# Four-tile dot products, a per-tile gather allowance and a rearranged end in a hard-max attention kernel

## Chip, cores, metric

One core of one Trainium2 chip. The metric is the device time of one execution in microseconds; medians are quoted. A ratio is the mean time of one kernel's fast runs over that of the other's fast runs of the same rounds, so it is not quite the ratio of the medians quoted beside it.

"Session" here means one set of runs made one after the other on one chip, with runs of the kernel before among them. Chips differed from session to session. A session in which the kernel before takes about 467 us is called **quick**, and one in which it takes over 500 us **late**. A run's label "fast" or "slow" is given against runs of the same kernel in the same session. All ratios below are taken within a session; where single figures of two sessions stand side by side, the runs are named.

## The reference

```python
# q, k, v: 4 x 4096 x 128, fp32
logits = np.matmul(q, k.transpose(0, 2, 1))
best = np.argmax(logits, axis=-1)
return v[b_idx, best, :]
```

For every query, find the key with the largest dot product and return that key's row of v.

## The kernel before

A tile is 128 queries; there are T = 128 tiles. For each tile, TensorE computes screening scores of groups of four keys (pd, psn), ScalarE turns them into A and E, VectorE folds them into W and takes the eight best (TOP). That gives one candidate group per query. GpSimd then gathers the group's three key differences (kg, 128 rows of 768 bytes), VectorE computes three dot products per query (prod, p1, p2, D), picks the best of the four keys (pick), and GpSimd gathers the row of v (vr), which is stored. Queries too close to call are flagged and recomputed exactly, once for tiles 0 to 63 within the loop and once for 64 to 127 at the end.

Each engine gets its own list of operations. The Python generators below only decide the order of these lists: a group's dots are placed into VectorE's list some tiles after its gathers went into GpSimd's list.

```python
# ... cut ...
def gather(c, t0, n):                     # n = 2 tiles
    # ... cut: cand_t[c] is allocated at a chunk's first tile
    x = cand_t[c][:, t0 - c0:t0 - c0 + n]
    nc.vector.tensor_scalar(out=x, in0=TOP.bitcast(U32)[:, t0:t0 + n, 0], ...)   # cand
    kg = rp.tile([P, n, 3, P], FP16, tag=f"kg{n}", name=f"kg_{t0}", bufs=8)
    for j in range(n):
        near_q.append(lambda j=j: nc.gpsimd.indirect_dma_start(out=kg[:, j]..., in_offset=IOA(ap=x[:, j:j + 1], axis=0)))
    near_q.append(mark)                   # mark: done.add(("kg", t0))
    start(dots(c, t0, n), "dots", c)

def dots(c, x, m):
    yield "until", lambda: ("kg", x) in done, 1 if x >= TAIL else 2     # tiles to wait after the mark
    nc.vector.tensor_tensor(out=prod, in0=kg, in1=natq[...], op=OP.mult)
    yield "dve",
    nc.vector.tensor_tensor(out=p1, in0=prod[:, :, :, 0:64], in1=prod[:, :, :, 64:128], op=OP.add)
    # ... cut: p2 alike, then D by tensor_reduce

def issue(it):                            # what GpSimd gets in tile it
    while near_q and (n < 1 + (it >= T - 28 and len(near_q) > 2) or near_q[0] in marks):
        ...                               # one kg gather (two near the end)
    # ... cut
    take_late(2 if n == 0 and len(late_q) > 4 or it >= T - 24 and it % 2 == 0 else 1)   # one vr gather

# ... cut: in tile it: screen, fold, step (one operation of each live generator), top, gathers(it - 3), step, issue
TAIL = T - 24
```

GpSimd's list is therefore kg, vr, kg, vr.

Of the kernel before, what the change touches and what calls it, by code (L numbers as in the profile page):

```python
# [20 lines left out]
QSCALE = 128.0  # L21
TAU = 8.0
NEAR = 0.5
LATE = 8


@with_exitstack
def kernel(ctx, tc, q, k, v, out):
# [202 lines left out]
    def top(t):  # L231
        nc.vector.max(out=TOP[:, t, :], in_=W_t[t % NW].bitcast(FP32))  # L232
# [6 lines left out]
    def gather(c, t0, n):  # L239
        c0, c1 = chunks[c]  # L240
        if t0 == c0:
            cand_t[c] = sp.tile([P, c1 - c0], U32, tag=f"cand{c1 - c0}", name=f"cand_{c}", bufs=6)
        x = cand_t[c][:, t0 - c0:t0 - c0 + n]
        nc.vector.tensor_scalar(out=x, in0=TOP.bitcast(U32)[:, t0:t0 + n, 0], scalar1=IDX, scalar2=IDX,
                                op0=OP.bitwise_and, op1=OP.bitwise_xor)
        kg = rp.tile([P, n, 3, P], FP16, tag=f"kg{n}", name=f"kg_{t0}", bufs=8)
        assert len(kg_t) < 8
        kg_t[t0] = kg
        for j in range(n):
            near_q.append(lambda j=j: nc.gpsimd.indirect_dma_start(  # L250
                out=kg[:, j].rearrange("p f d -> p (f d)"), out_offset=None, in_=k16[t0 // NQT],
                in_offset=IOA(ap=x[:, j:j + 1], axis=0)))
        mark = lambda: done.add(("kg", t0))
        marks.add(mark)
        near_q.append(mark)
        start(dots(c, t0, n), "dots", c)

    def dots(c, x, m):
        c0 = chunks[c][0]
        d = D_t[c % 4]  # L260
        b = x // NQT
        yield "until", lambda: ("kg", x) in done, 1 if x >= TAIL else 2
        kg = kg_t.pop(x)
        prod = rp.tile([P, m, 3, P], FP16, tag=f"prod{m}", name=f"prod_{x}")
        nc.vector.tensor_tensor(out=prod, in0=kg, in1=natq[b % 2][:, x - b * NQT:x - b * NQT + m, :].unsqueeze(2).to_broadcast([P, m, 3, P]),  # L265
                                op=OP.mult)
        yield "dve",
        p1 = rp.tile([P, m, 3, 64], FP16, tag=f"p1{m}", name=f"p1_{x}")
        nc.vector.tensor_tensor(out=p1, in0=prod[:, :, :, 0:64], in1=prod[:, :, :, 64:128], op=OP.add)  # L269
        yield "dve",  # L270
        p2 = rp.tile([P, m, 3, 32], FP16, tag=f"p2{m}", name=f"p2_{x}")
        nc.vector.tensor_tensor(out=p2, in0=p1[:, :, :, 0:32], in1=p1[:, :, :, 32:64], op=OP.add)  # L272
        yield "dve",
        nc.vector.tensor_reduce(out=d[:, x - c0:x - c0 + m, 1:4], in_=p2, axis=AX_X, op=OP.add)  # L274
        done.add(("dot", x))

    def pick(c, t0, t1):
        n = t1 - t0
        b, qt = t0 // NQT, t0 % NQT
        d = D_t[c % 4][:, 0:n, :]  # L280
        yield "until", lambda: all(("dot", x) in done for x in range(t0, t1, 2)), 0
        cand = cand_t.pop(c)
        mx = sp.tile([P, n, 1], FP32, tag=f"mx{n}", name=f"mx_{c}")
        nc.vector.tensor_reduce(out=mx[:, :, 0], in_=d, axis=AX_X, op=OP.max)
        yield "dve",
        near = sp.tile([P, n, 4], FP32, tag=f"near{n}", name=f"near_{c}")
        nc.vector.scalar_tensor_tensor(out=near, in0=d, scalar=NEAR, in1=mx.to_broadcast([P, n, 4]),
                                       op0=OP.add, op1=OP.is_ge)
        yield "dve",
        sel = sp.tile([P, n, 4], FP32, tag=f"sel{n}", name=f"sel_{c}")  # L290
        nc.vector.tensor_tensor(out=sel, in0=near, in1=iota8.unsqueeze(1).to_broadcast([P, n, 4]), op=OP.mult)
        yield "dve",
        nc.vector.tensor_reduce(out=CNT[:, t0:t1], in_=sel, axis=AX_X, op=OP.add)
        done.add(("cnt", c))
        yield "cnt",
        win = sp.tile([P, n], U32, tag=f"win{n}", name=f"win_{c}")
        nc.vector.scalar_tensor_tensor(out=win, in0=CNT[:, t0:t1], scalar=float(b * Sk - 8), in1=cand, op0=OP.add, op1=OP.add)
        for i in range(0, n, 4):
            put_values(c, i, n, win, out[b].rearrange("(p t) d -> p t d", p=P)[:, qt + i:qt + i + 4])
# [21 lines left out]
    def flag_segment(t0, t1, ready, stored):  # L321
# [41 lines left out]
        nc.vector.scalar_tensor_tensor(out=posn, in0=iota_r[:, 0:8], scalar=bs, in1=val, op0=OP.add, op1=OP.mult)  # L363
        yield "dve", 0.17
        OH = fp.tile([P, 8, P], BF16, tag="OH", name=f"OH_{t0}")
        nc.vector.tensor_tensor(out=OH, in0=iota_h.unsqueeze(1).to_broadcast([P, 8, P]),
                                in1=posn.unsqueeze(2).to_broadcast([P, 8, P]), op=OP.is_equal)
        yield "dve", 0.17
        rec2 = fp.tile([P, 8, 2], BF16, tag="rec2", name=f"rec2_{t0}")
        nc.vector.tensor_copy(out=rec2[:, :, 0], in_=e8)  # L370
        yield "dve", 0.17
# [269 lines left out]
    def step(it):  # L641
        quick = it >= TAIL
        waiting = [s for s in live if s["kind"] == "dots" and ready(s, it)]
        quota = 2 if len(waiting) > 1 else 1
        for s in list(live):
            if s["kind"] == "dots":
                if quota and advance(s, it, False):
                    quota -= 1
            else:
                if advance(s, it, False) and quick and s["kind"] == "pick" and s in live:  # L650
                    advance(s, it, False)

    rest = [0]
# [1 line left out]
    def take_late(n):  # L655
        while n > 0 and late_q:
            g = late_q.pop(0)
            n -= g not in stores
            g()
        while late_q and late_q[0] in stores:  # L660
            wait_q.append((clock[0] + 2, late_q.pop(0)))
# [7 lines left out]
    def issue(it):  # L669
        n = 0  # L670
        clock[0] = it
        put_out(it)
        while near_q and (n < 1 + (it >= T - 28 and len(near_q) > 2) or near_q[0] in marks):
            g = near_q.pop(0)
            n += g not in marks
            g()
        if fast and it >= rest[0]:
            fast.pop(0)()
            rest[0] = it + 3
        take_late(2 if n == 0 and len(late_q) > 4 or it >= T - 24 and it % 2 == 0 else 1)  # L680

    def gathers(t):
        for c, (t0, t1) in enumerate(chunks):
            if t0 <= t < t1 and ((t - t0) % 2 or t == t1 - 1):
                x = t0 + (t - t0) // 2 * 2
                gather(c, x, t - x + 1)
            if t == t0:
                start(pick(c, t0, t1), "pick", c)
        if t % 8 == 7:
            put_rec(t - 7, t + 1)  # L690
        if t == SEGS[1] - 1:
            last = [c for c, x in enumerate(chunks) if x[1] == t + 1][0]
            start(flag_segment(0, t + 1, lambda: ("cnt", last) in done, lambda: ("out", last) in done), "flags")

    TAIL = T - 24
    units = []
    for b in range(1, B):
        x = b * NQT
# [1 line left out]
    for it in range(T):  # L700
        b, qt = it // NQT, it % NQT
        if it < 8:
            load_part(1, it)
        elif 10 <= qt < 18:
            load_part(b + 1, qt - 2)
        elif 18 <= qt < 26:
            load_part(b + 2, qt - 18)
        open_units = [u for u in units if u[1] <= it]
        if open_units:
            u = min(open_units)  # L710
            units.remove(u)
            assert it <= u[0]
            u[2](*u[3:])
        if it == 1:
            turn_q(0, 4, 8)
        if it in (1, 2, 3):
            turn_q(0, it * 8, it * 8 + 8)
        elif qt >= 16 and qt % 2 == 0 and b + 1 < B:
            turn_q(b + 1, (qt - 16) * 2, (qt - 14) * 2)
        if it > 0:  # L720
            screen(it)
        if it >= 1:
            fold(it - 1)
        if it == 1:
            put_k(0, 1)
        if it % NQT in (9, 13):
            put_k(it // NQT + 1, it % NQT // 13)
        step(it)
        if it >= 2:
            top(it - 2)  # L730
        if 3 <= it <= TAIL:
            gathers(it - 3)
        if it >= TAIL:
            gathers(it - 2)
        step(it)
        issue(it)

    def flush():
        while near_q:
            near_q.pop(0)()  # L740
# [4 lines left out]

    screen(T)
    top(T - 2)
    fold(T - 1)
    top(T - 1)
    gathers(T - 2)  # L750
    gathers(T - 1)
    flush()
    assert not [s for s in live if s["kind"] == "flags"] and not fast
# [15 lines left out]
    for p in [s for s in live if s["kind"] == "pick"]:  # L769
        c = p["c"]  # L770
        dot = [s for s in live if s["kind"] == "dots" and s["c"] == c]
        while dot:
            two, dot = dot[:2], dot[2:]
            drain(two)
        last = c == len(chunks) - 1
        if last:
            flags_first(T // 2, T)
        drain([p], "cnt" if last else None)
    flags_last(T // 2, T, lambda: drain([p]), late_now)
    man.__exit__(None, None, None)  # L780
# [30 lines left out]
```

## Time and profile before

| | us |
|---|---|
| three timed runs | 506.16, 503.34, 513.95 |
| the profiled execution | 467.3 (span 465.5) |

These two rows do not fit together: the profile shows an execution 36 to 47 us faster than the timed runs.

From the page of before: the busy line, and the busy tenths of VectorE and the granted TensorE clock in 40 slices of the span.

```profile
PE 380.2 (82%) x1834; PEld 168.3 (36%) x1834; DVE 417.8 (90%) x825; ACT 376.8 (81%) x437; POOL 318.1 (68%) x345
...
DVE  2689999999999999999999999999998999998330
...
PEclk9999999999999999999999999999999999995555
```

VectorE is full from the fourth slice almost to the end, and the granted clock is full until the screening is done (1.00 to 418.3 us, 0.5 after that). The table of windows of before says the same by stage (columns: stretch and its length, busy us and instructions of PE, PEld, DVE, ACT and POOL, granted clock, DMA share, GB/s; PE is TensorE, DVE VectorE, ACT ScalarE, POOL GpSimd):

```profile
40.00:120.00 80.00, 76.63 (x378) 34.39 (x377) 80.00 (x135) 78.18 (x96) 53.52 (x59) 1.00 0.58 107
120.00:240.00 120.00, 112.72 (x550) 50.41 (x549) 118.23 (x202) 114.75 (x138) 89.96 (x95) 1.00 0.54 112
240.00:360.00 120.00, 107.05 (x500) 46.48 (x499) 117.72 (x236) 108.95 (x123) 89.91 (x90) 1.00 0.43 104
```

VectorE is busy 80.0 of 80 us, then 118.2 and 117.7 of 120; ScalarE and TensorE follow. The groups of instructions of before that matter (busy us, mean ns, then idle time of the engine just before them and what ended it):

```profile
L228 DVE SCALAR_TENSOR_TENSOR W<-psn,E 128x1024 int16<-128x1024 f32 x128 | 166.0, 1297 | 7.0 <-ACT E L215 5.5 <-PE psn L212 1.5
...
L250 POOL DMA_INDIRECT kg<-k,cand x128 | 127.4, 995 | 85.1 <-issue 26.6 <-DVE p L269 23.5 <-DVE cand L244 17.9
...
L265 DVE TENSOR_TENSOR prod<-kg,natq 128x768 f16<-128x768 f16 x64 | 34.9, 546 | 3.9 <-DMA kg<-k,cand 3.9
```

Keep two of these numbers in mind: W waits 7.0 us in all, and prod waits 3.9 us for the kg transfer. VectorE's timeline of before, late in the loop (start us, duration us, engine, line, operation), shows how its operations follow each other:

```profile
404.61 0.17 DVE L244 TENSOR_SCALAR cand<-TOP 128x2 uint32<-128x2 uint32 x1
404.68 0.34 DVE L274 TENSOR_REDUCE D<-p 128x6 f32<-128x192 f16 x1
404.95 1.30 DVE L228 SCALAR_TENSOR_TENSOR W<-psn,E 128x1024 int16<-128x1024 f32 x1
406.13 0.54 DVE L265 TENSOR_TENSOR prod<-kg,natq 128x768 f16<-128x768 f16 x1
406.60 1.22 DVE L232 MAX8 TOP<-W 128x8 f32<-128x1024 f32 x1
```

Start to start, W costs 1.18 us and prod 0.47. A fixed part of about 0.06 us per operation can be read from cand, which does next to nothing (404.61 to 404.68 here; start to start, 0.058 us is the most frequent value in this trace). That this is a fixed part is my estimate; the trace of after agrees with it: there p1 takes 0.265 us from start to start over two tiles and 0.464 over four (medians), 0.07 less than twice.

### The profile page before, as it was taken

Reading aid. Unit: us, or ns where it says so; the run is one execution under the profiler, and the core shown is the slowest. Engines: PE = TensorE matmul, PEld = TensorE weight load, DVE = VectorE, ACT = ScalarE, POOL = GpSimd, SP = SyncE. Lnnn points to the kernel's source line nnn. Section 1 sums busy time; section 2 is a strip of 40 time slices with the busy share of each in tenths; the row PEclk is TensorE's granted clock in tenths of the full one; section 3 lists DMA queues with packets and bytes.
Section 4 is the critical chain, followed back from the end, with each engine's and each line's share of the span. In section 5 each row is a group of like instructions: output and inputs, shape, how many; then the busy total and the mean of one; then the engine's idle time right before and its main releaser. Section 6 shows DMA issues by size and latency. Waiting matters only on the chain.

```text
span 465.5 us, 6396 instructions
## 1 busy us (share of the span) xinstructions
PE 380.2 (82%) x1834; PEld 168.3 (36%) x1834; DVE 417.8 (90%) x825; ACT 376.8 (81%) x437; POOL 318.1 (68%) x345
## 2 busy tenths in 40 slices
PE   8999999998999889999998889998998888850100
PEld 4444444443444344444443334443333333320000
DVE  2689999999999999999999999999998999998330
ACT  2999999999999989999997889999998888840000
POOL 8233557877677888776678876677777777767730
PEclk9999999999999999999999999999999999995555
DMA  7934576853325877943235653423432333322320
GB/s 130 227 66 96 107 103 97 139 120 85 80 76 135 148 140 128 121 126 81 79 98 137 129 116 94 100 80 87 110 101 79 86 86 99 87 71 68 94 74 4
DMA packets 43624, 47.54 MB, mean 102 GB/s; under 512 B 25000, under 2 KB 33451, under 8 KB 43584
## 3 DMA queue, kind: packets, MB, share of 16 engines
q0 software_dynamic: 18752, 30.97, 33.7%
q1 hardware_dynamic: 24832, 16.13, 13.1%
q8 instruction: 14, 0.23, 0.2%
q14 instruction: 26, 0.21, 0.2%
HBM read 39.59 MB, written 12.19 MB: 111 GB/s over the span
## 4 chain that ended last, share of the span: by engine, by line
DVE 31%; issue 23%; ACT 13%; PE 13%; DMA 9%; POOL 7%; POOLq 0%; DVEq 0%; ACTq 0%
DVE W L228 14%; ACT A L202 10%; PE psn L193 5%; DVE TOP L232 5%; PE psn L212 4%; DMA kg<-k,cand 4%; ACT E L215 4%; DMA vr<-in_v_dram,win 3%; DVE prod L265 3%; PE pd L193 3%; POOL kg L250 3%; POOL vr L304 2%; DVE D L274 2%; DVE p L269 2%; DMA natk<-in_k_dram 2%
## 5 line engine op out<-in xcount | busy, mean ns | idle before, releaser
L202 ACT ACTIVATE A<-pd 128x1024 f16<-128x1024 f32 x256 | 258.6, 1041 | 23.0 <-PE pd L193 22.7
L250 POOL DMA_INDIRECT kg<-k,cand x128 | 127.4, 995 | 85.1 <-issue 26.6
L228 DVE SCALAR_TENSOR_TENSOR W<-psn,E 128x1024 int16<-128x1024 f32 x128 | 166.0, 1297 | 7.0 <-ACT E L215 5.5
L193 PE MATMUL pd<-kT,qT 128*128 128x512 f16 x512 | 151.8, 378 | 15.7 <-ACT A L202 14.8
L193 PE MATMUL psn<-kT,qT 128*128 128x512 f16 x512 | 151.8, 378 | 15.3 <-ACT A L202 7.9
L304 POOL DMA_INDIRECT vr<-in_v_dram,win x128 | 136.6, 1067 | 39.0 <-issue 37.5
L193 PEld LDWEIGHTS <-qT 128*128 128x128 f16 x1024 | 98.4, 97 | 163.9 <-issue 76.0
L232 DVE MAX8 TOP<-W 128x8 f32<-128x1024 f32 x128 | 155.8, 1217 | 0.0
L212 PE MATMUL psn<-A,identh 128*128 128x512 f16 x512 | 152.1, 378 | 0.0
L215 ACT ACTIVATE E<-psn 128x1024 int16<-128x1024 f32 x128 | 132.2, 1033 | 5.0 <-PE psn L212 5.0
L212 PEld LDWEIGHTS <-identh 128*128 128x128 f16 x512 | 49.6, 97 | 60.8
L265 DVE TENSOR_TENSOR prod<-kg,natq 128x768 f16<-128x768 f16 x64 | 34.9, 546 | 3.9 <-DMA kg<-k,cand 3.9
L269 DVE TENSOR_TENSOR p<-prod 128x384 f16<-128x384 f16 x64 | 22.3, 349 | 0.1
L274 DVE TENSOR_REDUCE D<-p 128x6 f32<-128x192 f16 x64 | 21.5, 336 | 0.1
L173 ACT ACTIVATE kT<-uk 128x256 f16<-128x256 f32 x48 | 20.1, 419 | 0.9 <-PE uk L170 0.9
L64 POOL DMA_DIRECT2D natk<-in_k_dram x27 | 16.1, 599 | 0.9 <-POOLq L795 0.8
L67 POOL DMA_DIRECT2D natq<-in_q_dram x27 | 16.3, 605 | 0.2
L169 PE MATMUL uk<-identh,natk 128*128 128x128 f16 x96 | 15.8, 218 | 0.6 <-ACT A L202 0.6
L272 DVE TENSOR_TENSOR p<-p 128x192 f16<-128x192 f16 x64 | 15.7, 245 | 0.0
L464 PE MATMUL fp_e<-n_e,tri 128*128 128x1 f32 x2 | 0.6, 361 | 16.7 <-DVE n_e L462 16.7
L170 PEld LDWEIGHTS <-natk 128*128 128x128 f16 x96 | 9.3, 97 | 7.7 <-issue 5.3
L169 PEld LDWEIGHTS <-natk 128*128 128x128 f16 x96 | 9.3, 97 | 5.6
(147 smaller groups left out, 133.5 us busy)
## 6 DMA issues: line engine op xcount, KB each, us to landing
out_dram<-vr SPq DMA_DIRECT2D x32, 256.0 KB, 2.2
natq<-in_q_dram POOLq DMA_DIRECT2D x26, 128.0 KB, 3.2
k<-kd SPq DMA_DIRECT2D x8, 384.0 KB, 4.2
natk<-in_k_dram POOLq DMA_DIRECT2D x24, 128.0 KB, 3.9
kg<-k,cand POOLq DMA_INDIRECT x128, 2.8
vr<-in_v_dram,win POOLq DMA_INDIRECT x128, 2.8
natq<-in_q_dram POOLq DMA_DIRECT2D x1, 768.0 KB
natk<-in_k_dram POOLq DMA_DIRECT2D x1, 512.0 KB, 5.2
```

Source lines behind the costliest of these rows:

```text
L169: nc.tensor.matmul(out=o, lhsT=natk[b % 2][:, h, 4 * m + x, :], rhs=identh, start=True, stop=False)
L193: nc.tensor.matmul(out=ps[:, n * 512:(n + 1) * 512], lhsT=qT[b % 2][:, qt * P:(qt + 1) * P], rhs=kT[b % 2][:, u * 1024 + n * 512:u * 1024 ...
L202: nc.scalar.activation(out=A, in_=ps, func=AF.Abs)
L212: nc.tensor.matmul(out=ps[:, n * 512:(n + 1) * 512], lhsT=identh, rhs=A[:, n * 512:(n + 1) * 512], start=False, stop=True)
L215: nc.scalar.activation(out=E, in_=ps, func=AF.Relu, scale=QSCALE)
L228: nc.vector.scalar_tensor_tensor(out=W_t[t % NW].bitcast(I16)[:, 1::2], in0=ps, scalar=QSCALE, in1=E, op0=OP.mult, op1=OP.max)
L232: nc.vector.max(out=TOP[:, t, :], in_=W_t[t % NW].bitcast(FP32))
L250: near_q.append(lambda j=j: nc.gpsimd.indirect_dma_start(out=kg[:, j].rearrange("p f d -> p (f d)"), out_offset=None, in_=k16[t0 // NQT], ...
L265: nc.vector.tensor_tensor(out=prod, in0=kg, in1=natq[b % 2][:, x - b * NQT:x - b * NQT + m, :].unsqueeze(2).to_broadcast([P, m, 3, P]), op ...
L269: nc.vector.tensor_tensor(out=p1, in0=prod[:, :, :, 0:64], in1=prod[:, :, :, 64:128], op=OP.add)
L274: nc.vector.tensor_reduce(out=d[:, x - c0:x - c0 + m, 1:4], in_=p2, axis=AX_X, op=OP.add)
L304: late_q.append(lambda j=j: nc.gpsimd.indirect_dma_start(out=vr[:, j, :], out_offset=None, in_=v_flat, in_offset=IOA(ap=win[:, i + j:i + j ...
```

## The change

The intent: fewer fixed costs on the full engine, VectorE, by doing the dots of four tiles in one operation up to tile 72 (products still over two); with one dot operation of such a group per tile; an allowance per tile that lets GpSimd issue two kg gathers and as many vr gathers as fit; and a shorter end. The core of the diff:

```diff
-LATE = 8
+LATE = 7
+NKG = 6
@@ gather
-        kg = rp.tile([P, n, 3, P], FP16, tag=f"kg{n}", name=f"kg_{t0}", bufs=8)
+        kg = rp.tile([P, 4, 3, P], FP16, tag="kg", name=f"kg_{t0}", bufs=NKG)[:, 0:n]
@@ dots
-        yield "until", lambda: ("kg", x) in done, 1 if x >= TAIL else 2
+        gap = ("wait", 1) if m == 4 else ("dve",)
+        yield "until", lambda: ("kg", x) in done, 2 if m < 4 and x < TAIL else 1
-        nc.vector.tensor_tensor(out=prod, in0=kg, in1=natq[...], op=OP.mult)
-        yield "dve",
+        h = min(m, 2)
+        for i in range(0, m, h):
+            nc.vector.tensor_tensor(out=prod[:, i:i + h], in0=kg[:, i:i + h], in1=natq[...], op=OP.mult)
+            yield gap
@@ issue
-        while near_q and (n < 1 + (it >= T - 28 and len(near_q) > 2) or near_q[0] in marks):
+        while near_q and (n < 1 or near_q[0] in marks or it >= 16 and n < 2):
...
-        take_late(2 if n == 0 and len(late_q) > 4 or it >= T - 24 and it % 2 == 0 else 1)
+        if it < 16: ...
+        busy = 0.45 if 10 <= qt < 18 and b + 1 < B or 18 <= qt < 26 and b + 2 < B else 0.0
+        room[0] = min(room[0] + 2.35 - busy, 3.0) - n
+        while room[0] >= 1 and late_q:
+            take_late(1)
+            room[0] -= 1
@@ gathers
-            if t0 <= t < t1 and ((t - t0) % 2 or t == t1 - 1): ...
+            m = 4 if t1 <= T - 56 else 2 if t < T - 2 else 1
+            if t0 <= t < t1 and (t - t0) % m == m - 1:
+                gather(c, t - m + 1, m)
@@
-    TAIL = T - 24
+    TAIL = T - 38
@@ main loop: gathers now after the second step, always for tile it - 2
@@ cut: flag segment advanced twice per step, its OH in four pieces; the last chunk drained
@@      one group at a time, with the first flag operations moved ahead of its last two groups
```

More of the change, by code (lines that the diff above doesn't have):

```diff
@@ L245, in gather @@
                                 op0=OP.bitwise_and, op1=OP.bitwise_xor)
-        kg = rp.tile([P, n, 3, P], FP16, tag=f"kg{n}", name=f"kg_{t0}", bufs=8)
-        assert len(kg_t) < 8
+        kg = rp.tile([P, 4, 3, P], FP16, tag="kg", name=f"kg_{t0}", bufs=NKG)[:, 0:n]
+        assert len(kg_t) < NKG
         kg_t[t0] = kg
@@ L261, in dots @@
         b = x // NQT
-        yield "until", lambda: ("kg", x) in done, 1 if x >= TAIL else 2
+        gap = ("wait", 1) if m == 4 else ("dve",)
+        yield "until", lambda: ("kg", x) in done, 2 if m < 4 and x < TAIL else 1
         kg = kg_t.pop(x)
-        prod = rp.tile([P, m, 3, P], FP16, tag=f"prod{m}", name=f"prod_{x}")
-        nc.vector.tensor_tensor(out=prod, in0=kg, in1=natq[b % 2][:, x - b * NQT:x - b * NQT + m, :].unsqueeze(2).to_broadcast([P, m, 3, P]),
-                                op=OP.mult)
-        yield "dve",
-        p1 = rp.tile([P, m, 3, 64], FP16, tag=f"p1{m}", name=f"p1_{x}")
+        prod = rp.tile([P, 4, 3, P], FP16, tag="prod", name=f"prod_{x}")[:, 0:m]
+        h = min(m, 2)
+        for i in range(0, m, h):
+            nc.vector.tensor_tensor(out=prod[:, i:i + h], in0=kg[:, i:i + h],
+                                    in1=natq[b % 2][:, x + i - b * NQT:x + i + h - b * NQT, :].unsqueeze(2).to_broadcast([P, h, 3, P]),
+                                    op=OP.mult)
+            yield gap
+        p1 = rp.tile([P, 4, 3, 64], FP16, tag="p1", name=f"p1_{x}")[:, 0:m]
         nc.vector.tensor_tensor(out=p1, in0=prod[:, :, :, 0:64], in1=prod[:, :, :, 64:128], op=OP.add)
-        yield "dve",
-        p2 = rp.tile([P, m, 3, 32], FP16, tag=f"p2{m}", name=f"p2_{x}")
+        yield gap
+        p2 = rp.tile([P, 4, 3, 32], FP16, tag="p2", name=f"p2_{x}")[:, 0:m]
         nc.vector.tensor_tensor(out=p2, in0=p1[:, :, :, 0:32], in1=p1[:, :, :, 32:64], op=OP.add)
@@ L274, in dots @@
         nc.vector.tensor_reduce(out=d[:, x - c0:x - c0 + m, 1:4], in_=p2, axis=AX_X, op=OP.add)
-        done.add(("dot", x))
+        done.update(("dot", i) for i in range(x, x + m))
     def pick(c, t0, t1):
@@ L280, in pick @@
         d = D_t[c % 4][:, 0:n, :]
-        yield "until", lambda: all(("dot", x) in done for x in range(t0, t1, 2)), 0
+        yield "until", lambda: all(("dot", x) in done for x in range(t0, t1)), 0
         cand = cand_t.pop(c)
@@ L365, in flag_segment @@
         OH = fp.tile([P, 8, P], BF16, tag="OH", name=f"OH_{t0}")
-        nc.vector.tensor_tensor(out=OH, in0=iota_h.unsqueeze(1).to_broadcast([P, 8, P]),
-                                in1=posn.unsqueeze(2).to_broadcast([P, 8, P]), op=OP.is_equal)
-        yield "dve", 0.17
+        for z in range(4):
+            nc.vector.tensor_tensor(out=OH[:, 2 * z:2 * z + 2], in0=iota_h.unsqueeze(1).to_broadcast([P, 2, P]),
+                                    in1=posn[:, 2 * z:2 * z + 2].unsqueeze(2).to_broadcast([P, 2, P]), op=OP.is_equal)
+            yield "wait", 1
         rec2 = fp.tile([P, 8, 2], BF16, tag="rec2", name=f"rec2_{t0}")
@@ L649, in step @@
             else:
-                if advance(s, it, False) and quick and s["kind"] == "pick" and s in live:
+                if advance(s, it, False) and (quick or s["kind"] == "flags") and s in live:
                     advance(s, it, False)
@@ L678, in issue @@
             fast.pop(0)()
-            rest[0] = it + 3
-        take_late(2 if n == 0 and len(late_q) > 4 or it >= T - 24 and it % 2 == 0 else 1)
+            rest[0] = it + 2
+            n += 1
+        if it < 16:
+            take_late(2 if n == 0 and len(late_q) > 4 else 1)
+            return
+        b, qt = it // NQT, it % NQT
+        busy = 0.45 if 10 <= qt < 18 and b + 1 < B or 18 <= qt < 26 and b + 2 < B else 0.0
[3 more added lines that the diff above has]
+            room[0] -= 1
+    room = [0.0]
     def gathers(t):
         for c, (t0, t1) in enumerate(chunks):
-            if t0 <= t < t1 and ((t - t0) % 2 or t == t1 - 1):
-                x = t0 + (t - t0) // 2 * 2
-                gather(c, x, t - x + 1)
+            m = 4 if t1 <= T - 56 else 2 if t < T - 2 else 1
+            if t0 <= t < t1 and (t - t0) % m == m - 1:
+                gather(c, t - m + 1, m)
             if t == t0:
@@ L730 @@
             top(it - 2)
-        if 3 <= it <= TAIL:
-            gathers(it - 3)
-        if it >= TAIL:
+        step(it)
+        if it >= 2:
             gathers(it - 2)
-        step(it)
         issue(it)
@@ L747 @@
     top(T - 2)
+    gathers(T - 2)
+    flush()
     fold(T - 1)
     top(T - 1)
-    gathers(T - 2)
     gathers(T - 1)
@@ L771 @@
         dot = [s for s in live if s["kind"] == "dots" and s["c"] == c]
+        last = c == len(chunks) - 1
         while dot:
-            two, dot = dot[:2], dot[2:]
+            if last and len(dot) == 2:
+                flags_first(T // 2, T)
+            two, dot = (dot[:1], dot[1:]) if last else (dot[:2], dot[2:])
             drain(two)
-        last = c == len(chunks) - 1
-        if last:
-            flags_first(T // 2, T)
         drain([p], "cnt" if last else None)
```

## The prediction

> **What bounds it now.** In the table of windows (profile of before, 465.5 us) VectorE is busy 100% of 40 to 160 us and about 98% of 160 to 400; ScalarE is next (94 to 99% to 240 us), TensorE third at granted clock 1.00. In the timeline, W operations follow each other every 2.74 and 3.11 us in turn; eight tiles with their pick take 23.9 us, 2.99 per tile. That is VectorE's own work, start to start: W 1.19, TOP 1.14, and per pair of tiles prod 0.46, p1 0.26, p2 0.16, D 0.25, cand 0.06. ScalarE needs about 3 x 0.91 plus a key unit of about 0.3 every second tile, 2.9: little room beneath. The tail, last W at 418.8 to the end, is a serial chain: last gathers, dots, pick, flags, eight value gathers, FR, FK, FV, branch, store.
>
> The timed runs (503 to 514) are about 40 us slower than the profiled one (467.3). [...]
>
> **What changes.**
> 1. Tiles 0 to 71: four tiles cost 2 prod + one p1, p2, D, cand (0.92 + 0.46 + 0.26 + 0.45 + 0.06 = 2.15 us) instead of 2.38. Only four fixed costs of about 0.06 us go. Over 18 groups: -4 us of VectorE, on the path at full clock, nearly none if TensorE bounds.
> 2. GpSimd issues the same 256 gathers, in bursts, 1.31 us each: no gain in itself.
> 3. Tiles 90 to 125: dots follow their gather after two tiles instead of (mostly) three. From cand's start to the second gather's landing: 0.43 + 1.31 + 2.83 = 4.6 us (tail of the timeline). VectorE's work from cand to prod there: 4.0 us, 4.3 with a pick. So 0.3 to 0.6 us stall per pair, 18 pairs: +5 to +8 us at full clock; hidden if tiles take 3.3 us or more. Before's 2 to 3 us of kg stalls inside the loop should go.
> 4. End: tile 127 gathers alone, 126 earlier (-1.3), dots over one tile (-0.7), two flag operations before the wait (-0.7); seven instead of eight value gathers between last kg and FR. FR comes about 3 us earlier after the last W; one value gather now sits behind FV and gives 1.3 back: -1.5 to -3.
> 5. Flag segment twice as fast through the loop, its OH in four pieces: +0.2.
>
> Sum at full clock: -4 - 2.5 - 2 + 6.5 = about -2; with TensorE the bound: -2 to -5 (end, smoother VectorE).
>
> **Predicted: 502 us, range 493 to 511; faster by over 2% 0.14, within 2% 0.80, slower 0.06.**
>
> **Right or wrong in the profile.** W to W over tiles 20 to 70 falls from 2.99 to about 2.93; VectorE instructions fall by about 60; prod waits on the kg transfer in the last 40 tiles (several us, 3.9 before); last W to FR issue 13 to 14 us instead of 16.5; last W to end 44 to 45.
>
> **What would make it wrong.** Something else slowing the timed runs: if GpSimd or gather latency, bursts and the shorter distance cost much more; if small VectorE bursts stall TensorE there, the smoother order gains over 2%. Kg landing faster than 2.8 us would remove step 3's loss: 1.5% in the profile.

-4 (step 1), -2.5 (the kg stalls of before in the loop, step 3), -2 (the end, step 4) and +6.5 (step 3) make -2; the +0.2 of step 5 is not in it. The predicted 502 lies 4 us under 506, the median of the three timed runs.

## The result, and the profile after

| | before | after |
|---|---|---|
| median us, first session | 506.56 (4 runs) | 530.94 (4 runs, 528.53 to 534.28) |
| ratio | | 1.051, 95% interval 1.042 to 1.060 |
| profiled | 467.3 | 534.3 |

The change made the kernel 5% slower; 531 lies outside the predicted range, and the forecast was "within 2%". The profile after is of one of the timed runs, so it is of the late kind and must not be held against the quick profile of before without care. From the page of after, the lines that answer to those shown:

```profile
PE 398.8 (75%) x1834; PEld 171.1 (32%) x1834; DVE 419.3 (79%) x761; ACT 380.8 (72%) x437; POOL 311.8 (59%) x345
...
DVE  3679999747789989839799989684998598899420
...
PEclk9999999968999999969998999996999799996555
```

The same windows of after:

```profile
40.00:120.00 80.00, 69.19 (x323) 30.12 (x322) 69.71 (x94) 67.41 (x83) 50.76 (x56) 0.92 0.56 104
120.00:240.00 120.00, 100.16 (x462) 43.38 (x461) 98.69 (x137) 97.34 (x115) 74.18 (x80) 0.94 0.45 96
240.00:360.00 120.00, 98.59 (x465) 42.55 (x464) 106.51 (x201) 97.74 (x114) 71.70 (x75) 0.99 0.39 89
```

And the same groups of after:

```profile
L229 DVE SCALAR_TENSOR_TENSOR W<-psn,E 128x1024 int16<-128x1024 f32 x128 | 166.5, 1301 | 67.0 <-PE psn L213 31.8 <-PE pd L194 19.5 <-ACT E L216 8.9
...
L251 POOL DMA_INDIRECT kg<-k,cand x128 | 126.1, 985 | 149.3 <-DVE cand L245 119.5 <-issue 27.7 <-DMA kg<-k,cand 0.6
...
L269 DVE TENSOR_TENSOR prod<-kg,natq 128x768 f16<-128x768 f16 (+1 forms) x65 | 35.4, 545 | 4.9 <-DMA kg<-k,cand 3.9 <-issue 1.1
```

VectorE has as much work as before (419.3 us busy against 417.8) in a span 67 us longer. No engine is full any more: VectorE is busy 69.7 of 80 us, then 98.7 and 106.5 of 120. 60 of these 67 us stand in front of W, which waits 67.0 us instead of 7.0, for TensorE and ScalarE; prod waits less than 5 us. GpSimd's kg gathers are not slower (985 ns against 995), but they wait 119.5 us for cand instead of 17.9 (part of this belongs to the session: after waits 67.1 us for cand in a quick one, x5 below): with one cand for four tiles GpSimd pauses longer and then has a longer run of gathers. VectorE's instructions fell by 64, as predicted, and it did not matter.

What such a wait looks like, from the timeline of after (start us, duration us, engine, line, operation; the bracket gives the idle time before it and what ended it):

```profile
218.95 1.00 POOL L309 DMA_INDIRECT vr<-in_v_dram,win  x1 [0.30 <-issue]
...
220.25 1.07 POOL L309 DMA_INDIRECT vr<-in_v_dram,win  x1 [0.30 <-issue]
...
220.99 0.22 PE L171 MATMUL uk<-identn,natk 128*128 128x128 f16 x1
...
221.63 1.00 POOL L309 DMA_INDIRECT vr<-in_v_dram,win  x1 [0.30 <-issue]
...
222.94 0.96 POOL L251 DMA_INDIRECT kg<-k,cand  x1 [0.30 <-issue]
...
224.20 0.96 POOL L251 DMA_INDIRECT kg<-k,cand  x1 [0.30 <-issue]
...
225.47 1.16 POOL L251 DMA_INDIRECT kg<-k,cand  x1 [0.30 <-issue]
...
226.93 0.94 POOL L251 DMA_INDIRECT kg<-k,cand  x1 [0.30 <-issue]
228.18 1.00 POOL L309 DMA_INDIRECT vr<-in_v_dram,win  x1 [0.30 <-issue]
228.23 0.38 ACT L174 ACTIVATE kT<-uk 128x256 f16<-128x256 f32 x1 [6.00 <-remote]
228.66 1.01 PE L194 MATMUL pd<-kT,qT 128*128 128x512 f16 x2 [5.36 <-issue]
...
235.37 1.31 DVE L229 SCALAR_TENSOR_TENSOR W<-psn,E 128x1024 int16<-128x1024 f32 x1 [8.43 <-PE pd L194]
```

The last matmul into uk starts at 220.99 and is recorded with 0.22 us. ScalarE, idle for 6.00 us, takes uk up at 228.23, 7 us later ("remote": the profile found no releaser for it on this core). TensorE then waits for ScalarE and W for both; W is held up 8.43 us. Meanwhile GpSimd issues gathers one after the other, each 0.30 us after the end of the one before (starts at 218.95, 220.25, 221.63, 222.94, 224.20, 225.47, 226.93, 228.18). The matmul's own row shows nothing of the 7 us, so one must look at the recorded semaphore events instead. TensorE's recorded event nearest before ScalarE's start is at 228.20.

### The profile page after: what moved, and what is told of

It is laid out like the page before. It is cut to its first block, busy times and chain, and to the rows that moved or that the text cites. A ratio compares the mean times of both kernels' runs of the same rounds, so it can differ in the third digit from the quotient of the medians.

```text
span 532.4 us, 6319 instructions
## 1 busy us (share of the span) xinstructions
PE 398.8 (75%) x1834; PEld 171.1 (32%) x1834; DVE 419.3 (79%) x761; ACT 380.8 (72%) x437; POOL 311.8 (59%) x345
## 5 line engine op out<-in xcount | busy, mean ns | idle before, releaser
L251 POOL DMA_INDIRECT kg<-k,cand x128 | 126.1, 985 | 149.3 <-DVE cand L245 119.5
L194 PE MATMUL pd<-kT,qT 128*128 128x512 f16 x512 | 157.7, 391 | 45.8 <-issue 17.8
L194 PE MATMUL psn<-kT,qT 128*128 128x512 f16 x512 | 156.7, 388 | 32.0 <-ACT A L203 14.4
L194 PEld LDWEIGHTS <-qT 128*128 128x128 f16 x1024 | 100.1, 99 | 222.8 <-issue 141.7
L213 PE MATMUL psn<-A,identh 128*128 128x512 f16 x512 | 157.4, 390 | 0.0
L309 POOL DMA_INDIRECT vr<-in_v_dram,win x128 | 131.9, 1031 | 39.3 <-issue 38.1
L269 DVE TENSOR_TENSOR prod<-kg,natq 128x768 f16<-128x768 f16 (+1 forms) x65 | 35.4, 545 | 4.9 <-DMA kg<-k,cand 3.9
L274 DVE TENSOR_TENSOR p<-prod 128x384 f16<-128x384 f16 (+2 forms) x47 | 19.8, 422 | 0.1
L279 DVE TENSOR_REDUCE D<-p 128x6 f32<-128x192 f16 (+2 forms) x47 | 19.2, 411 | 0.1
L68 POOL DMA_DIRECT2D natq<-in_q_dram x27 | 16.2, 602 | 0.1
L277 DVE TENSOR_TENSOR p<-p 128x192 f16<-128x192 f16 (+2 forms) x47 | 13.3, 286 | 0.1
```

Of the source, the lines that this page charges most:

```text
L194: nc.tensor.matmul(out=ps[:, n * 512:(n + 1) * 512], lhsT=qT[b % 2][:, qt * P:(qt + 1) * P], rhs=kT[b % 2][:, u * 1024 + n * 512:u * 1024 ...
L213: nc.tensor.matmul(out=ps[:, n * 512:(n + 1) * 512], lhsT=identh, rhs=A[:, n * 512:(n + 1) * 512], start=False, stop=True)
L269: nc.vector.tensor_tensor(out=prod[:, i:i + h], in0=kg[:, i:i + h], in1=natq[b % 2][:, x + i - b * NQT:x + i + h - b * NQT, :].unsqueeze(2 ...
L309: late_q.append(lambda j=j: nc.gpsimd.indirect_dma_start(out=vr[:, j, :], out_offset=None, in_=v_flat, in_offset=IOA(ap=win[:, i + j:i + j ...
```

## The experiments

The candidates after the first result were three: the order in which GpSimd now gets its gathers (the allowance, the groups of four, or both); the shorter way between a gather and its dots; and the four-tile operations themselves, with their larger buffers. A fourth was that the loss was no property of the kernel but of the chip at that time.

Eighteen runs in eight sessions; all eighteen gave the correct result. In each table row, "before" is the kernel before in the same session.

### First session of experiments (quick): control and three mixtures

`x1_control`: before, unchanged.

> The kernel before, unchanged, to see its profile in the condition in which it takes 503 to 514 us (the profile on hand is of a 467 us execution). Theory S (late hand-overs): the 40 us lie in TensorE, ScalarE and VectorE waiting for each other although the instruction waited for has ended, as in the profile of after (W idle 67 us against 7): then this profile shows a span of about 505, a granted clock of 0.92 to 0.94, W idle of 30 to 45 us and fewer semaphore events than the 467 us one. Theory C (lower clock throughout): [...] matmuls of more than 0.216 us start to start. Time 503 to 508, ratio 0.99 to 1.01.

`x2_before_issue`: before, with `issue` of after (the allowance; the lines under `issue` in the diff above) and nothing else.

> Before with only the new gather allowance of GpSimd (two kg gathers per tile, room for value gathers). If the allowance (bunched gathers) costs the 25 us: 520 to 535. If the four-tile dots or the earlier dots cost it: 500 to 508.

`x3_after_old_issue`: after, with `issue` of before, the same edit the other way round:

```diff
-        while near_q and (n < 1 or near_q[0] in marks or it >= 16 and n < 2):
+        while near_q and (n < 1 + (it >= T - 28 and len(near_q) > 2) or near_q[0] in marks):
...
-        room[0] = min(room[0] + 2.35 - busy, 3.0) - n
-        while room[0] >= 1 and late_q: ...
+        take_late(2 if n == 0 and len(late_q) > 4 or it >= T - 24 and it % 2 == 0 else 1)
```

> After with the old gather allowance (one kg, one value gather per tile). If the allowance costs the 25 us: 500 to 508. If the four-tile dots or the shorter way from gather to dots cost it: 522 to 535.

`x4_after_pairs`, after with groups of two tiles everywhere:

```diff
-            m = 4 if t1 <= T - 56 else 2 if t < T - 2 else 1
+            m = 2 if t < T - 2 else 1
-NKG = 6
+NKG = 8
```

> After with dots of two tiles everywhere, the rest of the change kept. If grouping four tiles costs the 25 us: 500 to 508. If the allowance or the shorter way costs it: 522 to 535.

| | median us | before | ratio, 95% interval |
|---|---|---|---|
| x1_control | 466.53 | 467.74 | 0.999, 0.995 to 1.004 |
| x2_before_issue | 466.17 | 467.74 | 0.998, 0.994 to 1.001 |
| x3_after_old_issue | 464.53 | 467.74 | 0.993, 0.990 to 0.997 |
| x4_after_pairs | 472.98 | 467.74 | 1.011, 1.007 to 1.015 |

None of the expectations could be tested as written, because they assumed before at 506 and it took 468. What does follow: the 40 us are not the kernel's but the session's. And something in after costs 1% even here (x4); with the old allowance (x3) it does not.

### Second session (quick): the changed kernel again

`x5_after_again`, unchanged after.

> The changed kernel again, unchanged. If the 531 us came with the condition of that first session (in which before took 506), and before takes 467 here as in the last call: after takes 465 to 475, within 2% of before. If the loss belongs to the kernel in any condition: 485 to 495, ratio 1.04 to 1.06.

Measured: 476.66 us against 467.13, ratio 1.021 (1.018 to 1.025). So after loses 9.5 us in a quick session too. Its groups of instructions:

```profile
L229 DVE SCALAR_TENSOR_TENSOR W<-psn,E 128x1024 int16<-128x1024 f32 x128 | 165.9, 1296 | 8.1 <-ACT E L216 5.4 <-PE psn L213 2.3 <-PE pd L194 0.3
...
L269 DVE TENSOR_TENSOR prod<-kg,natq 128x768 f16<-128x768 f16 (+1 forms) x65 | 35.4, 545 | 10.3 <-DMA kg<-k,cand 9.7 <-issue 0.3
```

W waits 8.1 us, much as before; prod waits 10.3 us instead of 2.9 (x1) or 3.9 (the first profile). By tile, 7.1 us of it lie in tiles 94 to 126, as step 3 of the prediction has it, and 3.1 us in the four-tile groups, which it did not foresee. One such wait in the timeline of that run (start, duration, engine and operation; in the bracket the idle time before and what ended it):

```profile
365.06 0.16 DVE L245 TENSOR_SCALAR cand<-TOP 128x2 uint32<-128x2 uint32 x1
...
365.49 0.96 POOL L251 DMA_INDIRECT kg<-k,cand  x1 [0.39 <-DVE cand L245]
...
366.75 0.95 POOL L251 DMA_INDIRECT kg<-k,cand  x1 [0.30 <-issue]
...
367.93 1.30 DVE L229 SCALAR_TENSOR_TENSOR W<-psn,E 128x1024 int16<-128x1024 f32 x1
...
370.26 0.56 DVE L269 TENSOR_TENSOR prod<-kg,natq 128x768 f16<-128x768 f16 x1 [1.03 <-DMA kg<-k,cand]
```

cand starts at 365.06, the pair's first gather 0.43 us later and its second 1.69 us later. VectorE is through with W at 369.23 (367.93 + 1.30), finds prod next in its list, and stands for 1.03 us until the transfer has landed, 5.20 us after cand began. Between cand and prod it had only 4.17 us of other work.

This pointed to the distance between a gather and its dots, which after has cut from (mostly) three tiles to two. In time, from the start of cand to that of prod, for 14 pairs between tiles 94 and 123: 7.8 to 11.9 us in x1, 4.3 to 5.7 in x5. Two edits share in this: the line of `dots` below, and the allowance, which gives GpSimd both gathers of a pair in one tile.

### Third session (late): the distance, and the four-tile dots alone

`x6_after_wait2`, one line of after:

```diff
-        yield "until", lambda: ("kg", x) in done, 2 if m < 4 and x < TAIL else 1
+        yield "until", lambda: ("kg", x) in done, 2
```

> After with the dots of every group two tiles behind the mark of its last gather (before's distance) instead of one; all else as after. Theory K (in the calm sessions, before 467, after 477: the loss is VectorE waiting in prod for the kg transfer, 10.3 us against 2.9): the prod waits fall to under 4 us and the time to 466 to 470. Rival M (the multi-tile lumps and the gathers' order cost it, wherever dots stand): 474 to 478. In a session where before takes about 506 (late hand-overs): Theory B (bunched gathers hold up TensorE's completion signals): still over 520.

`x7_after_wait2_old_issue`: the same line, and `issue` of before.

> The last kernel with the old gather allowance too, the candidate for the best. Theory K: prod waits under 2 us, 460 to 464, better than before by about 1%. In a session of 506: under 506 if the bunched gathers are what hurts there.

`x8_before_fours`: before, with `dots` of after (the wait as in before), its kg buffers, and

```diff
-            if t0 <= t < t1 and ((t - t0) % 2 or t == t1 - 1): ...
+            m = 4 if t1 <= T - 56 else 2
+            if t0 <= t < t1 and (t - t0) % m == m - 1:
+                gather(c, t - m + 1, m)
```

> Before with the four-tile dots alone (tiles 0 to 71). My step 1 says -4 us: 462 to 465, W to W 2.92 to 2.93 us over tiles 24 to 40. If the saved fixed costs turn into ScalarE or TensorE waits: 466 to 468.

| | median us | before | ratio, 95% interval | W waits, us (profile) |
|---|---|---|---|---|
| x6_after_wait2 | 540.37 | 509.61 | 1.065, 1.054 to 1.075 | 79.7 |
| x7_after_wait2_old_issue | 529.57 (fast runs 524.05, 525.38) | 509.61 | none given: two of four runs were slow | 64.0 |
| x8_before_fours | 539.41 | 509.61 | 1.058, 1.046 to 1.070 | 85.3 |

The third session was late by chance. (The profile of x8 is of its slowest run, 544.18 us.) In x6 and x7 prod waits 0.0 us, and yet they lose 15 to 30 us: the distance is not what costs in late sessions. Four-tile dots with gathers by four, added to before (x8), cost all of it. The old allowance is worth about 15 us of the fast runs here (x6 539 to 543, x7 524 to 525), or 11 us by the means of all four runs, so the bunched gathers hurt too. Against the fast runs of before (mean 508.0), x7's two fast runs are 3.3% longer. My step 1, "-4 us", met +30.

x8 changes two things at once. VectorE's operations span four tiles, and cand is computed once for four tiles, so that GpSimd gets four tiles' gathers at a time and has to wait for VectorE half as often. The next session separates them.

### Fourth session (quick) and sixth (late): who computes for four, who gathers for four

`x9_fours_pair_gathers` is x8 with cand and the gathers of every two tiles; only the dots span four:

```diff
-    def gather(c, t0, n):
+    def gather(c, t0, n, i, k):           # tiles i to i+k of the group of n at t0
...                                        # cand over k tiles; kg allocated if i == 0
+        if i + k == n:                    # mark and dots when the group is whole
+            near_q.append(mark)
+            start(dots(c, t0, n), "dots", c)
...
+            if t0 <= t < t1 and (t - t0) % 2 == 1:
+                x = t - (t - t0) % m
+                gather(c, x, m, t - 1 - x, 2)
```

> The four-tile dots of the previous kernel (539 us where before took 507), but cand and the kg gathers of every two tiles as in before, so that GpSimd pauses for cand every two tiles. In a session of about 506: Theory B (runs of gathers without a pause hold up completion signals): near before, 503 to 515. Rival L (the four-tile VectorE operations or their buffers do it): 530 to 545. In a session of about 467: 462 to 466 for both (dots saved, cand not).

`x10_pairs_four_gathers` is the mirror: before's two-tile dots, one cand per four tiles up to tile 72, then two pairs of gathers and two groups of dots.

```diff
+        for i in range(0, n, 2):          # gather: after cand for n = 4 tiles
+            pair(c, t0 + i, y[:, i:i + 2])
+    def pair(c, t0, x):                   # before's kg of two tiles, its gathers, mark and dots
...
+            m = 4 if t1 <= T - 56 else 2
+            if t0 <= t < t1 and (t - t0) % m == m - 1:
+                gather(c, t - m + 1, m)
```

> Before with its two-tile dots, but one cand per four tiles, so that GpSimd gets gathers for four tiles at a time and pauses for cand half as often. In a session of about 506: Theory B: 525 to 545. Rival L: 503 to 512. In a session of about 467: 466 to 470 for both.

`x11_after_wait2_b` is x6 again, `x12_control_b` before again.

> After with dots two tiles behind their gathers' mark, again, because it fell into a 507 us session. In a session of about 467: Theory K: 466 to 470, prod waits under 4 us. Rival M: 474 to 478. In a session of about 506: 535 to 545 again.

> Before unchanged. In a session of about 506: its profile shows what its 40 us are: W idle of 30 to 50 us instead of 7, completion signals later the more gathers went before, half of the semaphore events missing. In a session of about 467: as the first control, ratio 0.99 to 1.01.

The fourth session was quick:

| | median us | before | ratio, 95% interval |
|---|---|---|---|
| x9_fours_pair_gathers | 465.53 | 467.30 | 0.996, 0.993 to 0.999 |
| x10_pairs_four_gathers | 467.31 | 467.30 | 1.000, 0.998 to 1.002 |
| x11_after_wait2_b | 464.83 | 467.30 | 0.995, 0.993 to 0.997 |
| x12_control_b | 467.69 | 467.30 | 1.001, 0.999 to 1.003 |

x11 settles the quick sessions. One tile more between gather and dots takes after from 477 to 465 us, and its prod no longer waits at all (the group of x11; the last number is the idle time):

```profile
L269 DVE TENSOR_TENSOR prod<-kg,natq 128x768 f16<-128x768 f16 (+1 forms) x65 | 35.3, 545 | 0.0
```

x3 of the first session shows a second way to the same end. It keeps the short wait after the mark, but its old allowance spreads a pair's gathers over two tiles, so that 7.4 to 10.6 us lie between cand and prod, and it took 464.53 us. Its prod, and then the W of x10, to be compared with late sessions:

```profile
L269 DVE TENSOR_TENSOR prod<-kg,natq 128x768 f16<-128x768 f16 (+1 forms) x65 | 35.2, 541 | 3.9 <-DMA kg<-k,cand 3.9
...
L228 DVE SCALAR_TENSOR_TENSOR W<-psn,E 128x1024 int16<-128x1024 f32 x128 | 166.0, 1297 | 7.2 <-ACT E L215 6.3 <-PE psn L212 0.8
```

The allowance alone (x2) brings prod to 4.6 to 4.9 us after cand late in the loop, but that is just enough, and prod waits 2.1 us in all. It is the allowance together with the rest of after that costs.

For x9 and x10 a late session was needed. `x13_fours_pair_gathers_b` missed it (quick again: 465.34 against 467.09, ratio 0.996); `x14_fours_pair_gathers_c` and `x15_pairs_four_gathers_b` met one.

> The four-tile dots with cand and kg gathers per two tiles, again, in the hope of a session of about 506. There, Theory B (runs of gathers without a pause): 503 to 515. Rival L (the four-tile VectorE operations or their buffers): 530 to 545. In a session of about 467: 463 to 467 again.

> As for the same kernel before. In a session of about 506: Theory B 503 to 515, Rival L 530 to 545. In a session of about 467: 463 to 467.

> Two-tile dots with one cand per four tiles, again. In a session of about 506: Theory B 525 to 545, Rival L 503 to 512. In a session of about 467: 466 to 470.

| late session | median us | before | ratio, 95% interval |
|---|---|---|---|
| x14: four-tile dots, gathers by two | 514.88 | 512.77 | 1.004, 0.994 to 1.014 |
| x15: two-tile dots, gathers by four | 541.44 | 512.77 | 1.055, 1.043 to 1.067 |

Together with before and x8 (the latter in its own late session, against its own runs of before) this is a full square. In the kernel before, whatever VectorE computes, it is the handing of gathers to GpSimd by four that costs 5 to 6% in a late session; by two it costs nothing that can be told from zero. Theory B stands, Rival L (the four-tile operations or their buffers) falls. The groups of x14:

```profile
L229 DVE SCALAR_TENSOR_TENSOR W<-psn,E 128x1024 int16<-128x1024 f32 x128 | 166.6, 1302 | 55.5 <-PE psn L213 32.7 <-PE pd L194 10.6 <-issue 6.5
...
L252 POOL DMA_INDIRECT kg<-k,cand x128 | 127.7, 997 | 130.1 <-DVE cand L245 61.6 <-issue 30.2 <-DVE near L294 14.2
```

And the same groups of x15:

```profile
L228 DVE SCALAR_TENSOR_TENSOR W<-psn,E 128x1024 int16<-128x1024 f32 x128 | 166.6, 1302 | 77.8 <-PE pd L193 29.2 <-PE psn L212 22.6 <-ACT E L215 12.5
...
L254 POOL DMA_INDIRECT kg<-k,cand x128 | 126.9, 991 | 152.8 <-DVE p L273 34.3 <-DVE cand L244 33.8 <-DVE near L291 33.3
```

The 27 us between the two profiled spans (513.8 and 540.4 us) are mostly the 22 us more that W waits in x15. The kg gathers themselves take as long in both (126.9 and 127.7 us), and the pauses before them are 23 us longer in x15. In the quick session the same two kernels' W waited 7.0 and 7.2 us.

### Seventh session (late): before itself, and a repair

`x17_control_c`, before unchanged, gave the profile that had been missing.

> Before unchanged. In a session of about 506: W idle 30 to 50 us instead of 7, TensorE's completion signals later the more gathers went before, about half of the semaphore events missing. In a session of about 467: as the other controls.

Measured: 512.97 us against 517.04 in the same session, ratio 0.997 (0.977 to 1.016). Its groups of instructions:

```profile
L228 DVE SCALAR_TENSOR_TENSOR W<-psn,E 128x1024 int16<-128x1024 f32 x128 | 166.6, 1301 | 49.6 <-PE pd L193 14.9 <-PE psn L212 13.6 <-ACT E L215 8.4
...
L250 POOL DMA_INDIRECT kg<-k,cand x128 | 126.8, 991 | 130.6 <-DVE p L269 33.0 <-issue 27.4 <-DVE cand L244 26.5
```

W waits 49.6 us instead of 7.0, again for TensorE and ScalarE, and the gathers are not slower (991 ns against 995); only the pauses before them grew with VectorE's. So before too pays in a late session, with the same kind of wait, and the change makes it longer. A lower clock throughout is not the reason: in this profile it is granted at 1.00 except in stretches of 3 to 14 us at 0.5 that come with stalls, 24 us in all before the last W. (The trace of after shows one such fall within a pause of 2.5 us: TensorE paused from 109.5 to 112.0 us, the clock was at 0.5 for 13.7 us from 110.9 us on, matmuls of 512 columns then started 0.43 us apart instead of 0.216, and W was held up 7.0 us until 116.6. So a stall costs something more than itself: TensorE is busy 390.5 us in x17, against 380.2 in x1, for the same matmuls.)

To see when TensorE's signals come, I took, from the recorded semaphore events, the time from the start of each matmul that signals to TensorE's next recorded event, against the number of gathers started in the 6.4 us before it. Mean ns (the first column of x1 rests on 5 matmuls):

| gathers in the last 6.4 us | 1 | 2 | 3 | 4 | 5 |
|---|---|---|---|---|---|
| x1, before, quick | 393 | 332 | 361 | 372 | 383 |
| x17, before, late | 415 | 467 | 697 | 910 | 1568 |
| x15, gathers by four, late | 423 | 470 | 549 | 838 | 1643 |
| after, late | 401 | 570 | 544 | 840 | 1158 |

In a quick session the signal comes after 0.33 to 0.39 us whatever GpSimd does. In a late one it is by and large the later, the more densely gathers went before. One caution: the late profiles have recorded only about half of all semaphore events (4,604 in x17, 4,540 in after, against 8,655 in x1), and of TensorE's own 447 of 603. A missing event makes the next one look late, so the sizes are too large. A second count needs no event: the time from the start of the last matmul into pd to the A that ScalarE makes of it, where ScalarE had been idle. In quick sessions (x1, x5, x10) its median is 0.47 to 0.48 us with three, four and five gathers alike. In late ones it is 0.47 us with four gathers too, but with five, which is an unbroken run, it is 1.59 us in x17 (16 cases), 3.02 in x15 (20) and 2.32 in after (26). Such runs are what the hand-over by four adds: of the 248 gathers before the last W, 68 stand in runs of six or more in x17 and as many in x14, but 130 in x15 and 118 in after. In x1, which is quick, 117 do and nothing comes late, so dense gathers alone are not enough.

In every late profile the first 24 tiles run as in a quick one (2.90 and 3.17 us per tile over the first and second eight in x17 as in x1), and the stalls begin near 100 us.

`x16_repaired` puts both findings into after: cand and gathers by two tiles, `issue` of before, dots two tiles behind the mark.

```diff
-        yield "until", lambda: ("kg", x) in done, 2 if m < 4 and x < TAIL else 1
+        yield "until", lambda: ("kg", x) in done, 2
...                                        # issue as in x3, gather as in x9
-            if t0 <= t < t1 and (t - t0) % m == m - 1:
-                gather(c, t - m + 1, m)
+            h = min(m, 2)
+            if t0 <= t < t1 and (t - t0) % h == h - 1:
+                x = t - (t - t0) % m
+                gather(c, x, m, t - h + 1 - x, h)
```

> A repair: after with cand and kg gathers of every two tiles (GpSimd pauses as in before), with the old gather allowance, and dots two tiles behind the mark everywhere. In a session of about 467: 461 to 465. In a session of about 506: 500 to 512, no worse than before.

It took 521.74 us against 517.04, ratio 1.020 (1.006 to 1.033): the 5% are gone, but it is not better than before, and the expectation (500 to 512) was missed. `x18_repaired_b`, the eighth session, was quick:

> The repaired version again. In a session of about 467: 461 to 465, faster than before by 0.5 to 1.3%. In a session of about 506 to 517: within 3% of before again.

Measured: 466.71 us against 467.29, ratio 0.998 (0.995 to 1.002). The expected 461 to 465 was missed too. No version was found that beats before in both kinds of session. x3 (-0.7%) and x11 (-0.5%) are the best in quick ones; x11 is among the worst in late ones (+6%, as x6), and x3 was not run in one. Why x18 gives back x11's 2 us was not looked into; prod waits 0.0 us in both, and W to W over tiles 24 to 40 is 3.00 us against 2.95.

## Why the prediction was wrong

1. **What bounds it.** For quick sessions it was right: VectorE is full. I saw that the timed runs were 40 us slower than the profile and offered one explanation, a lower TensorE clock with TensorE as the bound; no trace showed it. The late traces disagree: in after, matmuls of 512 columns mostly still start 0.216 us apart (0.43 where the clock is 0.5), and the clock is 1.00 or, around stalls, 0.5. In late sessions no engine is the bound (the busiest, VectorE, is busy 79% of the span of after); the hand-overs between engines are.
2. **Step 2 is the step that failed**: "GpSimd issues the same 256 gathers, in bursts, 1.31 us each: no gain in itself." I counted the gathers and their pitch, and treated their order as free. It is free in quick sessions (x10: 1.000). In late ones handing them over by four costs 5.5% alone (x15: +29 us), where four-tile dots with gathers by two cost 0.4%, not to be told from zero (x14). The new allowance costs 11 to 15 us more in a kernel that gathers by four (x6 against x7). The prediction was measured in a late session. These parts do not add up to the loss of after, which is 24 us: with the old allowance and the longer distance, after loses 3.3% with gathers by four (x7, two fast runs) and 2.0% by two (x16, another session). How the loss of after itself divides between the two stays open. Under "what would make it wrong" I had named GpSimd as a possible culprit, but gave the whole upper side too little weight: 6%.
3. **Step 3 was right in mechanism and about right in size.** Predicted 0.3 to 0.6 us per pair from tile 90 on, 5 to 8 us; measured 7.1 us in tiles 94 to 126 (x5), unevenly: single waits reach 1.5 us. What it missed are 3.1 us in the four-tile groups, whose last two gathers also stand closer to their prod. Restoring the distance is worth 12 us (x5 476.7, x11 464.8, each against before at 467), and so is the old allowance (x3 464.5, against before at 468), which restores it too; I had not counted the allowance as part of the distance. In the late session the term is hidden, as it said it would be with longer tiles: prod waits 4.9 us in after.
4. **Step 1 was right in rate, too large in total.** W to W over tiles 24 to 40 became 2.92 us in x3 (2.93 predicted, 2.99 before). In after itself (x5) it stayed at 2.99, and over the stretch that I had named, tiles 20 to 70, it is 3.05 in x1, 3.00 in x3 and 3.08 in x5. In total the dots are worth 2 to 3 us, not 4 (x9 -1.8 us, with cand still by pairs; x3 -3.2 us with everything but the allowance).
5. **Step 4 was half right.** (FR, FK and FV are GpSimd's gathers for the flagged queries at the end: their records, rows of k and rows of v.) From the last W to FR went from 16.2 us (x1) to 14.4 (x5); 13 to 14 was predicted. FR then waited for VectorE's flag chain, not for GpSimd (it stood 0.97 us idle). The way from the last W to the end did not shrink to 44 to 45 us: 47.5 against 46.4. The last FK row came 1.6 us late for its dots, and the vr gather behind FV put the last scatter at 36.4 instead of 35.3 us after the last W.
6. **The sum.** In quick sessions -2 was predicted and +9.5 measured: prod waits +7.4 (10.3 against 2.9; I had reckoned +4 net), the end +1.1 (I had -2), and the rest, with the dots' saving of which little is left, about +1 (I had -4). In the late session of the prediction 24.4 us were lost. These terms do not carry over to it: prod waits 4.9 us there, and what grew is the wait of W, by 60 us against the quick profile of before and by 17 us against the late one (x17, 49.6).

Shown: that the hand-over by four causes a loss of 5.5% in the kernel before in a late session (mirror pair, one session), and that the short distance causes the loss in quick ones (x11, one line). Argued only: that the way there is the unbroken run of gathers delaying completion signals. The correlation, the count without events and the idle times fit it, but no run changed the signals' lateness alone.

Open: what makes a session late. The three late sessions among the experiments ran on three different chips, so it is not one bad chip, and none of the three was met in a quick session. It is also open whether the recording of events itself is part of it, since the late profiles lose half of them and no run is known to be free of recording. The two come together in time: in x17 the events are nearly complete for the first 60 us (807, against 840 in x1), thin out from 60 to 80 us (278 against 390), and are fewest from 100 to 120 us (93 against 401), where the stalls have begun. Which brings the other, or whether a third thing brings both, no run here shows. And the cost of the new allowance without four-tile gathers (x2, x4) was never seen in a late session.

## What to carry to other kernels

If a profile and the timed runs differ by more than their scatter, first get a profile of the slow kind; a plan built on the fast one answers another question. When an operation is batched on a full engine, ask what the same batching does to the engine that it feeds: here VectorE saved 0.06 to 0.08 us per operation (cand, p1, p2 and D in after), while GpSimd got twice the work at a time and half the pauses. And a consumer placed closer to an asynchronous transfer needs the whole latency counted (0.43 + 1.31 + 2.8 us in the prediction; 0.43 + 1.26 + 3.51 in the wait shown for x5) against the work that lies between.
